# Identity copies on GpSimd, the first maxima at every fifth value step, and the SSD output steps between product and convolution, in a two-layer diffusion backbone

## The chip, the cores and the metric

The kernel runs on one core of a Trainium2 chip. A core has a matrix engine (TensorE, PE in the profile; its weight loads are PEld), a vector engine (VectorE, DVE), an engine for activations (ScalarE, ACT), a general engine (GpSimd, POOL) and one that issues most DMAs (SyncE, SP). Each works through its own queue of instructions in order and waits on semaphores for the others. The metric is the device time of one execution in microseconds.

## The reference

One batch of 512 latent tokens and 256 context tokens, width 1024, passes through two layers. Every sub-layer is preceded by an RMS norm and an adaptive shift and scale, and closed by a gate, all from a condition vector.

```python
h_l = modulate(rms_norm(x, norm_mix_w[i]), mod_l[0], mod_l[1])
...
o_l, o_c = attention_mixer(h_l, h_c, ...)     # layer 0
o_l, o_c = mamba2_mixer(h_l, h_c, ...)        # layer 1
x = x + mod_l[2] * o_l
h_l = modulate(rms_norm(x, norm_ffn_w[i]), mod_l[3], mod_l[4])
x = x + mod_l[5] * conv_ffn(h_l, ...)
```

Layer 0 mixes by attention: 16 query heads of 64 on 4 key heads, norm on queries and keys, softmax over latent and context keys. Layer 1 mixes by a Mamba-2 state-space scan (SSD) in both directions, with 8 groups of 4 heads and a state of 128:

```python
xbc = silu(dwconv_centred(xbc, conv_w, conv_b))      # 5 taps; x, B and C
states = einsum('bcsgn,bcsgrp->bcgrpn', bc, xw)      # per chunk of 128 tokens
cb = einsum('bcqgn,bcsgn->bcqsg', cc, bc)
w = cb[..., None] * decay * dtc[:, :, None]
y = einsum('...', w, xc) + einsum('bcqgn,bcgrpn->bcqgrp', cc, h_in) * exp(acs)
y = y + d_skip * xs;  out = rms_norm(y * silu(z), norm_w) @ w_out
```

Each layer ends with a gated feed-forward network with a convolution of width 3.

## The kernel before

Activations lie transposed, channels on the 128 partitions and the 768 tokens along the free axis. Every fp32 product is three matmuls on a high and a low half of each operand (`mm3`, lines 99 to 109: high by high L105, high by low L106, low by high L108). `load_w` (L90 to L96) fetches a weight tile by a DMA from SP (L95, `wst`), rounds it on ScalarE (L85, `wh`) and subtracts on VectorE or GpSimd (L87, `wl`); these tiles share a pool of ten buffers, so about three loads are under way. PSUM has two double banks (`S`) and four banks (`Bank`) that all products share: a product can start when the reader of the bank's former content is done.

Each engine's order is set by the tile framework: instructions are ranked by their place in the program and put on their engine when their operands are planned to be ready; a block at the start of attention (`manual_schedule`) keeps PE, ScalarE and VectorE in program order. DMAs are issued by SP in its own order.

**Start.** SP issues X (four DMAs, L1254), the parameters, the modulation weights (L122), the first weight slabs (L412) and the constants `cst` (L421). PE warms up (L431). ScalarE squares the eight tiles of X (L435), VectorE adds them (L437), PE sums over partitions (L236, `ssa`), an inverse root follows (L239 to L247, `rba`), PE spreads it over partitions with the identity from `cst` (L253, `rsTa`), the tokens are modulated (L281, `ht`; L290 and L291, `hha` and `hla`), and the first slab matmul `ps_l` starts. The modulation comes from `ps_ada` (L128). Slabs are split into `wsh` (ScalarE) and `wsl` (GpSimd).

**Attention, first maxima.** Softmax subtracts a bound: the maxima of the scores per query. `maxima` (L586 to L621) computes them for a pair of heads in seven steps: matmuls `ps_m` (L596), a reduction on VectorE (L598), and at the end minima `mz` (L614) and a diagonal matrix `diag` (L619), made with the two copies `id2` of the identity (L576). The scores `ps_s` (L668) then get the bound by one more matmul, `diag` by ones (L670), and go to ScalarE's exponential (L671). For the first pair, the steps of `maxima` are interleaved with the matmuls of the values (`ps_v`, L515; three per step `i` of the loop at L727). For the later pairs they are interleaved with the scores of the pair before.

**SSD.** For each of eight groups, `inproj` (L959 to L978) makes, one after the other, two tiles of x, then B, C and two of z: a product over 8 blocks (`gemm`, `ps_in`), and for x, B and C `conv`: ScalarE copies the product to `raw` (L947, L949) and makes the middle tap with bias (L950), VectorE adds four taps (L952), ScalarE applies SiLU (L953). `core` (L984 to L1105) does the group's scan as a generator: transposes of x (`ps_xt`, L992) and of B (L999), weighting (`xw`, L1006), `ps_cb` (L1037) and first state (`ps_st`, L1018), DMAs of decay rows (`E`, L1050) with exponentials on ScalarE (L1055, L1057) and products on GpSimd and VectorE (L1059, L1061, L1067), the other states, and then for each of two halves `pr` an output step: DMAs `ec` (L1076), `ps_yo` (L1083), its product with `ec` on VectorE (L1085), an add on GpSimd (L1086), `ps_y` (L1092), its reading by VectorE (L1095, into the tile `xf`), the sum (L1096), the gate (L1097, `z`), the square (L1099) and its sum (L1103). The loop at L1108 advances the group before (`prev`) while the present one is projected: its remaining states and E products after the first x, output step 0 after the B convolution, output step 1 after the C convolution; the present group's own `core` starts behind that.

Of the kernel before, what the change touches and what calls it, by code (L numbers as in the profile page):

```python
# [11 lines left out]
ALU = mybir.AluOpType  # L12
AX = mybir.AxisListType
PSUM = bass.MemoryType.PSUM
# [4 lines left out]
C = 256  # L19
# [48 lines left out]
def t3(g, name, dt=F32, n=T):  # L68
    return g.t3p.tile([P, n], dt, tag="t3", bufs=g.n3, name=name)
# [232 lines left out]
def S(g, name):  # L302
    return g.ps.tile([P, 1024], F32, tag="S", bufs=2, name=name)


def Bank(g, name):
    return g.ps.tile([P, 512], F32, tag="B", bufs=4, name=name)
# [71 lines left out]
def attention(g, fill, X, late):  # L379


    nc, I = g.nc, g.I
    S64 = slice(0, 64), slice(64, 128)
    Bk, Sb = (lambda name: Bank(g, name)), (lambda name: S(g, name))
    t2 = lambda name, dt=F32: g.t3p.tile([P, 512], dt, tag="t2", bufs=6, name=name)
# [115 lines left out]
    raw = [t3(g, f"raw{j}") for j in range(6)]  # L501
# [71 lines left out]
    nc.scalar.copy(onesr, g.ones)  # L573
    id2 = g.const.tile([P, HD], F32, name="id2")
    for h in S64:
        nc.scalar.copy(id2[h], g.ident[h, h])  # L576
    small = lambda name, dt=F32: g.p.tile([P, 2, T // P], dt, tag="mx", bufs=4, name=name)

    class Pair:
# [109 lines left out]
    for n, j in enumerate((0, 1, 2, 4, 5, 3)):  # L689
        ps = Bk("ps_c")  # L690
# [34 lines left out]

    m = pairs[0].maxima()
    for i, _ in enumerate(vals):  # L727
        if i % 6 == 5:
            next(m, None)
            next(qgen[1], None)  # L730
    for _ in m:
        pass
# [1 line left out]
    for p in range(NH // 2):  # L734
        m = iter(())
        if p < 7:
# [3 lines left out]
            m = pairs[p + 1].maxima()  # L740
# [129 lines left out]
def ssd(g, x, norm, wf, bg, close):  # L870


    nc, I, tc = g.nc, g.I, g.tc
    par = lambda name, j, rows=P: g.par[:rows, PC[name] + j : PC[name] + j + 1]
    h = norm.h
# [11 lines left out]
    t3 = lambda g, nm, dt=F32: g.t3p.tile([P, TW], dt, tag="t3", bufs=g.n3, name=nm)  # L887
    t2 = lambda nm, dt=F32, n=512: g.t3p.tile([P, n], dt, tag="t2", bufs=39, name=nm)
    small = lambda nm, shape: g.t3p.tile(shape, F32, name=nm)
    tok = lambda t: slice(t * P + (2 if t >= 4 else 0), (t + 1) * P + (2 if t >= 4 else 0))  # L890
    def gemm(w, streams):
        ps = S(g, "ps_in")
        for _ in gemm_in(g, [(ps, w)], h, (0, L), [[(i, 0, (L, C)[i])] for i in streams]):
            pass
        return ps
# [3 lines left out]
    ps = ps_dt  # L899
# [27 lines left out]
    for i in range(0, P, H2):  # L927
        f, b = slice(i, i + 32), slice(i + 32, i + 64)
# [11 lines left out]
            nc.vector.memset(r[:, c0 : c0 + 2], 0.0)  # L940
    raw_n = [0]

    def conv(ps, j, both, cv):
        raw = raws[raw_n[0] % 2]
        raw_n[0] += 1
        n = TW if both else L
        nc.scalar.copy(raw[:, 2 : 2 + L], ps[:, :L])  # L947
        if both:
            nc.scalar.copy(raw[:, L + 4 : L + 4 + C], ps[:, L:T])  # L949
        nc.scalar.activation(cv, raw[:, 2 : 2 + n], AF.Identity, scale=par("sw2", j), bias=par("sb", j))  # L950
        for tap in (0, 1, 3, 4):
            nc.vector.scalar_tensor_tensor(cv, raw[:, tap : tap + n], par(f"sw{tap}", j), cv, ALU.mult, ALU.add)  # L952
        follow(g, nc.scalar.activation(cv, cv, AF.Silu))  # L953
        return cv

# [3 lines left out]
    def inproj(gi):  # L959

        G = Group()
        ld = lambda i: load_w(g, I["win"][6 * gi + i])
        G.x = []
        for j in range(2):
            ps = ps_x0 if gi == j == 0 else gemm(ld(j), (1, 0))
            G.x.append(conv(ps, 2 * gi + j, True, t3(g, "xf")))
            yield G
        G.B = conv(gemm(ld(2), (1, 0)), 16 + gi, True, t3(g, "Bf"))
        yield G
        G.C = conv(gemm(ld(3), (0,)), 24 + gi, False, t2("Cf"))  # L970
        yield G
        G.z = []
        for j in range(2):
            ps = gemm(ld(4 + j), (0,))
            z = t2("z")
            follow(g, nc.scalar.activation(z, ps[:, :L], AF.Silu))
            G.z.append(z)
            yield G  # L978
# [5 lines left out]
    def core(gi, G):  # L984
# [25 lines left out]
        st = []  # L1010
# [58 lines left out]
        for pr in range(2):  # L1069

            ec = []
            for d in range(2):
                e = t2("ec")
                for k in range(2):
                    row = d * 32 + 4 * gi + 2 * pr + k
                    nc.sync.dma_start(e[64 * k : 64 * k + 64], ead[row : row + 1, :].broadcast_to([64, L]))  # L1076
                ec.append(e)
            for d in range(2):
                po = Bank(g, "ps_yo")
                for c in range(4):  # L1080
                    s = st[3 - c if d else c]
                    c0 = d * 256 + pr * P
                    nc.tensor.matmul(po[:, c * P : (c + 1) * P], s[:, c0 : c0 + P], G.C[:, c * P : (c + 1) * P],  # L1083
                                     start=True, stop=True)
                nc.vector.tensor_tensor(ec[d], ec[d], po, ALU.mult)  # L1085
            nc.gpsimd.tensor_tensor(ec[0], ec[0], ec[1], ALU.add)  # L1086
            py = Bank(g, "ps_y")
            for c in range(4):
                cs = slice(c * P, (c + 1) * P)
                for e in range(2):  # L1090
                    r = 2 * pr + e
                    nc.tensor.matmul(py[64 * e : 64 * e + 64, cs], xt[:, c, r * HD : (r + 1) * HD], W[r][:, cs],  # L1092
                                     start=True, stop=True)
            y = G.x[pr][:, :L]
            nc.vector.scalar_tensor_tensor(y, y, par("sd", 2 * gi + pr), py, ALU.mult, ALU.add)  # L1095
            nc.vector.tensor_tensor(y, y, ec[0], ALU.add)  # L1096
            nc.vector.tensor_tensor(G.z[pr], G.z[pr], y, ALU.mult)  # L1097
            sq = t2("ysq")
            nc.scalar.activation(sq, G.z[pr], AF.Square)  # L1099
            if acc[0] is None:  # L1100
                acc[0] = sq
            else:
                nc.gpsimd.tensor_tensor(acc[0], acc[0], sq, ALU.add)  # L1103
            gated.append(G.z[pr])
            yield  # L1105

    prev = iter(())
    for gi in range(8):  # L1108
        for i, G in enumerate(inproj(gi)):
            if i in (0, 2, 3):  # L1110
                next(prev, None)
            if gi == 0 and i == 3:
                nt = T // P
                acsT, dtT = small("acsT", [P, nt, H2]), small("dtT", [P, nt, H2])
                for src, dst in ((acs, acsT), (dt, dtT)):
                    pt = Bank(g, "ps_dtT")[:, : nt * H2]
                    for t in range(nt // 2):
                        nc.tensor.transpose(pt[:, t * P : (t + 1) * P], src[:, t * P : (t + 1) * P], g.ident)
                    nc.vector.tensor_copy(dst.rearrange("p (a c) h -> p c a h", a=2),
                                          pt.rearrange("p (c a h) -> p c a h", c=nt // 2, a=2))  # L1120

                pe = Bank(g, "ps_end")
                for d, row in ((0, P - 1), (1, 0)):
                    nc.tensor.matmul(pe[:, d * nt * 32 : (d + 1) * nt * 32], g.ident[:, row : row + 1].broadcast_to([P, P]),
                                     acsT[:, :, d * 32 : (d + 1) * 32], start=True, stop=True)
                pev = pe[:, : nt * H2].rearrange("p (d t h) -> p d t h", d=2, t=nt)

                dec = small("dec", [P, 4, 2, 32])
                steps = [(5, 4)] + [(i, 3 - i) for i in range(3)]
                for i, (tf, tb) in enumerate(steps):  # L1130
                    follow(g, nc.scalar.activation(dec[:, i, 0], pev[:, 0, tf], AF.Exp))
                    follow(g, nc.scalar.activation(dec[:, i, 1], pev[:, 1, tb], AF.Exp))

                dw = small("dw", [P, nt, H2])
                for d in range(2):
                    hs = slice(d * 32, d * 32 + 32)
                    nc.vector.tensor_tensor(dw[:, :, hs], pev[:, d], acsT[:, :, hs], ALU.subtract)
                follow(g, nc.scalar.activation(dw, dw, AF.Exp))
                nc.vector.tensor_tensor(dw, dw, dtT, ALU.mult)

                for d, t in enumerate((4, 5)):
                    hs = slice(d * 32, d * 32 + 32)
                    nc.vector.tensor_tensor(dw[:, t, hs], dw[:, t, hs], dec[:, 0, d], ALU.mult)
                nacs = small("nacs", [P, 4, H2])
                nc.vector.tensor_scalar(nacs, acsT[:, :4], -1.0, None, ALU.mult)
            if i == 3:
                cur = core(gi, G)
            if i >= 3:
                next(cur)
        prev = cur  # L1150
# [25 lines left out]
    po = [S(g, "ps_wo") for _ in range(2)]  # L1176
# [10 lines left out]
    for kp in range(8):  # L1187
        w = load_w(g, I["wout0"][kp])
        if kp == 4:
            ws, ps = wm(4), Bank(g, "ps_wo")  # L1190
# [19 lines left out]
    for m in range(4, KT):  # L1210
# [5 lines left out]
        for seg in SEGS[0] if m == KT - 1 else [(0, 0, L)]:  # L1216
            _, a, b = seg
            if m > 4:
                ps = Bank(g, "ps_wo")[:, : b - a]
# [10 lines left out]
    first = first_tiles(g, wf, nxt, bg)  # L1230
# [195 lines left out]
```

## Time and profile before

| | us |
|---|---|
| runs | 1956.39, 1950.32, 1954.3 |
| median | 1954.3 |
| profiled execution | 1954.1 |
| its span, first to last instruction | 1952.0 |
| PE busy | 1890.7 |
| VectorE, ScalarE, GpSimd busy | 1343.8, 825.4, 295.6 |

The profiled execution's clock of TensorE was 0.987 of full speed in the mean. In the views below, a timeline row gives start, duration, engine, line, operation, the tile written and the tiles read, and in brackets how long the engine had been idle before and what ended that. A row of waits gives total, number and longest. A row of windows gives for a stretch its length, then the busy time of PE, PEld, VectorE, ScalarE and GpSimd with the number of instructions, the granted clock, the share of the DMA engines, and GB/s.

### The profile page before, as it was taken

The page shows a single profiled execution, that of the slowest core. Times are in us where ns is not written, and L with a number is a line of the kernel's source. Part 1 is how long each engine was busy: PE and PEld are TensorE (multiplying, and loading weights), DVE is VectorE, ACT ScalarE, POOL GpSimd, SP SyncE. Part 2 cuts the span into 40 slices and gives each one's busy share as a digit, 9 for nine tenths or more (in the row PEclk, how much of TensorE's full clock was granted, in tenths as well). Part 3 has the DMA queues.
Part 4 walks back from the last instruction along what each step waited for, and adds up shares of the span by engine and source line. Part 5 has one row for each costly group of instructions (what it writes and reads, how often), then busy time and mean ns, then how long its engine had stood idle before and what let it go on. Part 6 is the DMA issues. An engine that isn't in the chain of part 4 may idle for free.

```text
span 1952.0 us, 27591 instructions
## 1 busy us (share of the span) xinstructions
PE 1890.7 (97%) x10844; PEld 1555.9 (80%) x10844; DVE 1343.8 (69%) x1994; ACT 825.4 (42%) x1428; POOL 295.6 (15%) x272
## 2 busy tenths in 40 slices
PE   6999999999999999999999999999999999999999
PEld 5776554678888888888888888878888888888887
DVE  4478777767777777775588876667878465555555
ACT  3444443345222222222256776665667253333331
POOL 1332110022000000000040333332335210000000
PEclk8989999999999999999999999999999999999999
DMA  8221316103333444421123334343254322323332
GB/s 330 67 80 53 119 63 215 44 23 143 127 127 123 130 130 130 130 82 60 65 87 99 102 119 120 108 119 106 78 162 121 107 69 94 98 97 97 98 97 87
DMA packets 73425, 210.02 MB, mean 108 GB/s; under 512 B 8912, under 2 KB 14416, under 8 KB 73168
## 3 DMA queue, kind: packets, MB, share of 16 engines
q1 hardware_dynamic: 73296, 208.26, 33.4%
q8 instruction: 85, 1.39, 0.3%
q14 instruction: 44, 0.36, 0.1%
HBM read 198.79 MB, written 6.82 MB: 105 GB/s over the span
## 4 chain that ended last, share of the span: by engine, by line
PE 66%; DVE 15%; issue 6%; POOL 3%; DMA 3%; ACT 2%; SPq 1%; POOLq 0%; DVEq 0%; ACTq 0%
PE ps_up L105 10%; PE ps_up L106 10%; PE ps_up L108 10%; PE ps_d L105 6%; PE ps_d L108 6%; PE ps_d L106 6%; DVE xf L952 2%; PE ps_s L668 2%; PE ps_o L632 2%; DVE E L1061 1%; DVE Bf L952 1%; DMA E<-ad 1%; DVE wl L87 1%; DVE ht L281 1%; PE ps_wo L105 1%
## 5 line engine op out<-in xcount | busy, mean ns | idle before, releaser
L87 DVE TENSOR_TENSOR wl<-wst,wh 128x1024 fp32r<-128x1024 f32 x205 | 254.0, 1239 | 276.2 <-PE ps_up L106 119.7
L85 ACT CAST wh<-wst 128x1024 fp32r<-128x1024 f32 x211 | 221.0, 1048 | 434.8 <-DMA wst<-in_wup 327.7
L106 PE MATMUL ps_up<-hlf,wh 128*128 128x512 f32 x1008 | 357.0, 354 | 0.0
L105 PE MATMUL ps_up<-hhf,wh 128*128 128x512 f32 x1008 | 357.0, 354 | 0.0
L108 PE MATMUL ps_up<-hhf,wl 128*128 128x512 f32 x1008 | 356.8, 354 | 0.0
L105 PEld LDWEIGHTS ps_up<-hhf,wh 128*128 128x128 f32 x1008 | 190.5, 189 | 26.2
L106 PEld LDWEIGHTS ps_up<-hlf,wh 128*128 128x128 f32 x1008 | 190.6, 189 | 26.1
L108 PEld LDWEIGHTS ps_up<-hhf,wl 128*128 128x128 f32 x1008 | 190.5, 189 | 26.1
L105 PE MATMUL ps_in<-hhs,wh 128*128 128x512 f32 (+1 forms) x560 | 206.0, 368 | 0.0
L108 PE MATMUL ps_in<-hhs,wl 128*128 128x512 f32 (+1 forms) x560 | 201.1, 359 | 0.0
L106 PE MATMUL ps_in<-hls,wh 128*128 128x512 f32 (+1 forms) x560 | 200.3, 358 | 0.0
L105 PE MATMUL ps_d<-hdh,wh 128*128 128x512 f32 (+1 forms) x568 | 193.9, 343 | 1.0 <-DVE X L778 0.8
L108 PE MATMUL ps_d<-hdh,wl 128*128 128x512 f32 (+1 forms) x568 | 193.5, 341 | 0.0
L106 PE MATMUL ps_d<-hdl,wh 128*128 128x512 f32 (+1 forms) x568 | 193.0, 340 | 0.3 <-DVE hdl L87 0.3
L778 DVE SCALAR_TENSOR_TENSOR X<-ps_d,mod,X 128x512 f32<-128x512 f32 (+1 forms) x240 | 132.4, 583 | 22.2 <-PE ps_d L108 21.8
L105 PEld LDWEIGHTS ps_in<-hhs,wh 128*128 128x128 f32 x560 | 107.1, 191 | 15.3 <-issue 1.2
L106 PEld LDWEIGHTS ps_d<-hdl,wh 128*128 128x128 f32 x568 | 106.7, 188 | 15.4 <-DVE hdl L87 0.7
L108 PEld LDWEIGHTS ps_in<-hhs,wl 128*128 128x128 f32 x560 | 106.8, 191 | 15.2
L105 PEld LDWEIGHTS ps_d<-hdh,wh 128*128 128x128 f32 x568 | 106.3, 188 | 15.1 <-DVE X L778 1.3
L106 PEld LDWEIGHTS ps_in<-hls,wh 128*128 128x128 f32 x560 | 107.0, 191 | 13.9
L167 DVE SCALAR_TENSOR_TENSOR junk<-wada,cb 128x1024 f32<-128x1024 f32 x96 | 116.6, 1215 | 1.1 <-ACT cb L159 0.9
L108 PEld LDWEIGHTS ps_d<-hdh,wl 128*128 128x128 f32 x568 | 106.7, 188 | 13.3
(340 smaller groups left out, 3523.7 us busy)
## 6 DMA issues: line engine op xcount, KB each, us to landing
wst<-in_wup SPq DMA_DIRECT2D x88, 512.0 KB, 3.6
wada<-in_adaT SPq DMA_DIRECT2D x48, 512.0 KB, 3.5
wst<-in_win SPq DMA_DIRECT2D x48, 512.0 KB, 3.7
wst<-in_wdown SPq DMA_DIRECT2D x44, 512.0 KB, 4.2
wada<-in_adaB SPq DMA_DIRECT2D x32, 512.0 KB, 5.0
E<-ad SPq DMA_DIRECT2D x64, 256.0 KB, 6.9
ec<-ead SPq DMA_DIRECT2D x64, 128.0 KB, 4.4
wst<-in_wout SPq DMA_DIRECT2D x16, 512.0 KB, 3.6
```

Source lines behind the costliest of these rows:

```text
L85: keep(nc.scalar.copy(hi, src))
L87: keep(eng.tensor_tensor(lo, src, _r(hi), ALU.subtract))
L105: mm(out, wh, ah, start=first, stop=False)
L106: mm(out, wh, al, start=False, stop=False)
L108: mm(out, wl, ah, start=False, stop=last)
L167: g.tc.keep_in_program_order(nc.vector.scalar_tensor_tensor(junk, w, 1.0, cb[:, v * D : (v + 1) * D], ALU.mult, ALU.mult, accum_out=md[:, ...
L281: nc.vector.scalar_tensor_tensor(t[:, c0:c1], ap, g.moda[layer][ca][:, m, v : v + 1], rs[:, c0:c1], ALU.mult, ALU.mult)
L632: nc.tensor.matmul(po[S64[e], :n], v, pr[:, 512 * e + off : 512 * e + off + n], start=first, stop=last)
L668: nc.tensor.matmul(outs[e], a[S64[e], k], b[S64[e], q], start=i == 0, stop=False)
L778: nc.vector.scalar_tensor_tensor(ap, o[:, c0:c1], gate[:, m, v : v + 1], ap, ALU.mult, ALU.add)
L952: nc.vector.scalar_tensor_tensor(cv, raw[:, tap : tap + n], par(f"sw{tap}", j), cv, ALU.mult, ALU.add)
L1061: nc.vector.tensor_tensor(E[0], E[0], E[1], ALU.add)
```

## The change

Three edits. First, the two copies of the identity (L576) go from ScalarE to GpSimd. Second, the steps of the first pair's maxima are taken at every fifth step of the values, from the first on, and no longer at every sixth; the steps of the query preparation stay at every sixth. Third, in the SSD `inproj` stops between product and convolution of B and of C as well, and the output steps of the group before are taken there. The VectorE instructions of these steps that read PSUM are collected in `late`, and the next tap of a convolution that is written gets them as predecessors in VectorE's order (no semaphore).

```diff
     for h in S64:
-        nc.scalar.copy(id2[h], g.ident[h, h])
+        nc.gpsimd.tensor_copy(id2[h], g.ident[h, h])
...
     for i, _ in enumerate(vals):
+        if i % 5 == 0:
+            next(m, None)
         if i % 6 == 5:
-            next(m, None)
             next(qgen[1], None)
...
         for tap in (0, 1, 3, 4):
-            nc.vector.scalar_tensor_tensor(cv, raw[:, tap : tap + n], par(f"sw{tap}", j), cv, ALU.mult, ALU.add)
+            i = nc.vector.scalar_tensor_tensor(cv, raw[:, tap : tap + n], par(f"sw{tap}", j), cv, ALU.mult, ALU.add)
+            while late:
+                g.tc.add_manual_dep(i.ins, late.pop().ins.name, mybir.DependencyInfo(
+                    mybir.DependencyClass.NoSync, mybir.DependencyReason.DATA), reason="PSUM first")
...
-        G.B = conv(gemm(ld(2), (1, 0)), 16 + gi, True, t3(g, "Bf"))
-        yield G
-        G.C = conv(gemm(ld(3), (0,)), 24 + gi, False, t2("Cf"))
-        yield G
+        for name, i, st in (("B", 2, (1, 0)), ("C", 3, (0,))):
+            ps = gemm(ld(i), st)
+            yield None
+            setattr(G, name, conv(ps, 8 * i + gi, i == 2, t3(g, "Bf") if i == 2 else t2("Cf")))
+            yield G
...
-                nc.vector.tensor_tensor(ec[d], ec[d], po, ALU.mult)
+                late.append(nc.vector.tensor_tensor(ec[d], ec[d], po, ALU.mult))
...
-            nc.vector.scalar_tensor_tensor(y, y, par("sd", 2 * gi + pr), py, ALU.mult, ALU.add)
+            late.append(nc.vector.scalar_tensor_tensor(y, y, par("sd", 2 * gi + pr), py, ALU.mult, ALU.add))
...
-        for i, G in enumerate(inproj(gi)):
-            if i in (0, 2, 3):
+        i = -1
+        for G in inproj(gi):
+            if G is None:
+                next(prev, None)
+                continue
+            i += 1
+            if i == 0:
                 next(prev, None)
```

On ScalarE, at the start of the program; `id` are the two copies, `acc` and `sql` the squares of X:

```order
 L573 CAST onesr<-ones 128x128
-L576 COPY id_731<-cst 64x64 x2
 L435 ACTIVATE acc<-X 128x512
 L435 ACTIVATE sql<-X 128x512 x7
```

On GpSimd, at the start of the program after the change; the second `ISA` is the library instruction, `wsl` the low half of a slab:

```order
L1428 MEMSET const-uint8-127 128x1
L1434 UNCONDITIONAL_BRANCH
L576 COPY id_731<-cst 64x64 x2
L87 ISA
L87 TENSOR_TENSOR wsl<-wst,wsh 128x768 x6
```

The copies left the place ahead of the squares and stand ahead of GpSimd's library instruction and its first `wsl`.

On PE in attention, before: the last maxima matmuls of the first pair, with value matmuls around them (18 of them between `ps_m` and `ps_s`):

```order
L515 MATMUL ps_v<-wh,hla_1_121 128x256
L596 MATMUL ps_m<-kh_948,qh 128x256 x4
L515 MATMUL ps_v<-wh,hha_2_122 128x256
...
L515 MATMUL ps_v<-wh,hla_7_133 128x256
L668 MATMUL ps_s<-qh,kh_948 128x512 x2
L668 MATMUL ps_s<-qh,kl_949 128x512 x2
L668 MATMUL ps_s<-ql,kh_948 128x512 x2
L670 MATMUL ps_s<-diag_1221,onesr 128x512 x2
```

The same place after (51 value matmuls between `ps_m` and `ps_s`):

```order
L515 MATMUL ps_v<-wh,hla_6_115 128x256
L596 MATMUL ps_m<-kh_948,qh 128x256 x4
L515 MATMUL ps_v<-wh,hha_7_116 128x256
...
L515 MATMUL ps_v<-wh,hla_7_133 128x256
L668 MATMUL ps_s<-qh,kh_948 128x512 x2
L668 MATMUL ps_s<-qh,kl_949 128x512 x2
L668 MATMUL ps_s<-ql,kh_948 128x512 x2
L670 MATMUL ps_s<-diag_1184,onesr 128x512 x2
```

The maxima stand 33 value matmuls earlier; from `ps_s` on the order is the same.

On VectorE in a steady SSD group, before, from the second half of B's taps to the weighting; the `xf` row with `ps_y` is output step 1 reading its PSUM bank:

```order
L952 SCALAR_TENSOR_TENSOR Bf<-raw_9472,par,Bf 128x770
L87 TENSOR_TENSOR wl<-wst,wh 128x1024
L952 SCALAR_TENSOR_TENSOR Bf<-raw_9472,par,Bf 128x770
L952 SCALAR_TENSOR_TENSOR Cf<-raw_9473,par,Cf 128x512 x2
L1095 SCALAR_TENSOR_TENSOR xf<-xf,par,ps_y 128x512
L952 SCALAR_TENSOR_TENSOR Cf<-raw_9473,par,Cf 128x512
L87 TENSOR_TENSOR wl<-wst,wh 128x1024
L952 SCALAR_TENSOR_TENSOR Cf<-raw_9473,par,Cf 128x512
L1085 TENSOR_TENSOR ec<-ec,ps_yo 128x512 x2
L1096 TENSOR_TENSOR xf<-xf,ec 128x512
L1097 TENSOR_TENSOR z<-z,xf 128x512
```

The same place after (one more `wl` stands some rows above it):

```order
L87 TENSOR_TENSOR wl<-wst,wh 128x1024
L955 SCALAR_TENSOR_TENSOR Bf<-raw_9472,par,Bf 128x770
L1102 SCALAR_TENSOR_TENSOR xf<-xf,par,ps_y 128x512
L1092 TENSOR_TENSOR ec<-ec,ps_yo 128x512 x2
L1103 TENSOR_TENSOR xf<-xf,ec 128x512
L1104 TENSOR_TENSOR z<-z,xf 128x512
L87 TENSOR_TENSOR wl<-wst,wh 128x1024
L955 SCALAR_TENSOR_TENSOR Cf<-raw_9473,par,Cf 128x512 x2
L1013 TENSOR_TENSOR xw<-xt,dw 128x512
L955 SCALAR_TENSOR_TENSOR Cf<-raw_9473,par,Cf 128x512
```

Output step 1 stands ahead of all taps of C instead of between them, and the taps of C are mixed with the weighting `xw`. On SP one weight load moves from ahead of the second group's E rows to behind them, and so for all later groups. PE's order in the SSD is the same but for the place of the x transposes, which stand one matmul earlier.

More of the change, by code (lines that the diff above doesn't have):

```diff
@@ L941, in ssd @@
     raw_n = [0]
+    late = []
     def conv(ps, j, both, cv):
```

## The prediction

> **What bounds the kernel now.** I read the page first, then the waits of PE, then each place where PE stood, instruction by instruction, with the granted clock around it.
>
> ```profile
> PE 1890.7 (97%) x10844; PEld 1555.9 (80%) x10844; DVE 1343.8 (69%) x1994; ACT 825.4 (42%) x1428; POOL 295.6 (15%) x272
> PE ps_xt L992 <- DVE xf L1095: 13.8, 6, 3.8
> PE ssa L236 <- DVE qn L440: 12.3, 1, 12.3
> PE ps_s L670 <- DVE diag L619: 3.6, 3, 3.1
> PE ps_first L106 <- POOL hlf L288: 2.8, 5, 1.0
> ```
>
> PE is busy for 97% of the span, so without removing matmuls only two things can shorten this kernel: PE's waits, and the stretches at a lower clock. The last four lines are the longest waits (us in total, times, longest one). The first three are the places that the three edits touch; the fourth and all smaller ones are not touched. The profiled execution took 1954.1 us, 2.1 more than its span; the median of the runs is 1954.3, so I sum against 1954.1 and take the result for the median. About 0.3% (6 us) is what a measurement of this kernel can tell from no change.
>
> **Start: the identity copies leave ScalarE.** The timeline of the first 30 us (start, duration, engine, line, in brackets the idle time before and who ended it), and two groups of DMAs with the median from issue to landing last:
>
> ```profile
> 0.74 1.98 SPq L1254 DMA_DIRECT2D X<-in_xT  x4
> 7.45 2.40 SPq L122 DMA_DIRECT2D wada<-in_adaA  x3
> 13.90 0.50 ACT L576 COPY id<-cst 64x64 f32<-64x64 f32 x2 [11.58 <-DMA cst<-in_cst]
> 14.41 0.63 ACT L435 ACTIVATE acc<-X 128x512 f32<-128x512 f32 x1
> 14.94 3.73 ACT L435 ACTIVATE sql<-X 128x512 f32<-128x512 f32 x7
> 15.59 5.47 DVE L437 TENSOR_TENSOR acc<-acc,sql 128x512 f32<-128x512 f32 x7 [14.32 <-ACT sql L435]
> 21.12 1.87 PE L236 MATMUL ssa<-ones,acc 128*128 128x1 f32 x8 [12.26 <-DVE qn L440]
> 24.46 1.99 POOL L87 TENSOR_TENSOR wsl<-wst,wsh 128x768 fp32r<-128x768 f32 x1 [24.02 <-ACT wsh L85]
> 24.83 1.11 PE L253 MATMUL rsTa<-cst,rba 128*128 128x128 f32 x4
> 26.37 1.07 PE L128 MATMUL ps_ada<-wada,sc 128*32 128x256 f32 x16
> 28.49 0.49 PE L105 MATMUL ps_l<-hha,wsh 128*128 128x512 f32 x1 [1.05 <-ACT hha L290]
> 29.64 0.63 PE L108 MATMUL ps_l<-hha,wsl 128*128 128x512 f32 x1
> 12.00:26.00 14.00, 4.88 (x30) 3.54 (x31) 7.02 (x16) 5.99 (x14) 1.54 (x1) 0.52 1.05 389
> X<-in_xT SPq DMA_DIRECT2D x4, 512.0 KB, 5.1
> wada<-in_adaA SPq DMA_DIRECT2D x11, 384.0 KB, 8.1
> ```
>
> ScalarE stands until 13.90 for the constants. Behind its two copies stand, one after the other, the squares of X, their sum on VectorE (ends at 15.59 + 5.47 = 21.06), the row sums `ssa` on PE, the norm and the first slab matmul at 28.49. X itself came long before: four DMAs, issued from 0.74 to 2.72; with the median of 5.1 the first piece is there at about 5.8 and the last at 7.8. Without the copies the first add can start two squares later, at 5.8 + 0.63 + 0.53 (3.73 / 7) = 7.0 by that median, a little over 1 us sooner if the first piece, alone on the queues, lands faster than the median; seven adds of 0.78 (5.47 / 7) then end between 11.3 and 12.5. The last piece with its two squares and one add would allow 9.7, so the adds decide. I take 11.5: 21.06 - 11.5 = **9.6 us earlier**, bounds 8.5 and 10.5.
>
> What is late next? The constants hold the identity for the transposes `rsTa` too; they land at 13.9, and `rsTa` moves to 24.83 - 9.6 = 15.2. The second block of modulation weights, issued from 7.45 to 9.85, lands by about 9.85 + 8.1 = 18.0 at the latest; its matmuls move to 26.37 - 9.6 = 16.8, and the slab behind them to 18.9, so they may be up to 1 us late: that is in the bounds. The clock was 0.52 from 12 to 26; I assume that the moved work meets the same (a gain of up to 3 otherwise).
>
> On GpSimd the copies now wait for 13.9 instead, ahead of a library instruction that has no row, and ahead of `wsl`. That `wsl` is wanted by the third slab matmul, at 29.64 - 9.6 = 20.0; with 1.99 for itself it must start by 18.0. The copies are done at 13.9 + 1.0 (twice ScalarE's 0.50) = 14.9, so 3 us are left for the library. Its price lies between zero and a delay that eats all 9.6; I take zero, since this row of the trace shows `wsl` starting without delay behind the same instruction, though there it had long idle time. Term: **-9.6**.
>
> **The first maxima.** The chain of waits (first row), the timeline and the windows, 115 to 142 us:
>
> ```profile
> 115.68 2.35 PE ps_v L515 x18
> 124.04 1.22 DVE L598 TENSOR_REDUCE mb<-ps_m 128x4 f32<-128x1024 f32 x1 [1.55 <-PE ps_m L596]
> 129.25 1.03 DVE L619 TENSOR_TENSOR diag<-id,mz 128x384 fp32r<-128x384 f32 x2
> 130.33 0.50 PE L670 MATMUL ps_s<-diag,onesr 64*128 64x512 f32 x2 [3.11 <-DVE diag L619]
> 132.00:142.00 10.00, 10.00 (x43) 5.82 (x46) 7.57 (x12) 5.93 (x10) 3.61 (x3) 0.50 0.29 85
> ```
>
> When the last maxima matmul is done (124.04) VectorE needs until 130.3 for reduction, minima and diagonal: 6.3 us. PE has 18 value matmuls left for that time (2.35 us as in the first row) and six score matmuls, then stands 3.11. In the new order 51 value matmuls follow the last maxima; 33 more at 0.13 (2.35 / 18) are 4.3 us of cover against 3.1 of wait, which goes whole. The last row says that PE, never idle from 132 to 142, had half its clock there: up to 5 us lost. ScalarE's exponentials between the matmuls would keep some of it, so I take 4 (bounds 0 and 5). Moving the maxima forward costs PE nothing: their number is the same, and `diag` is ready early. Term: 3.1 + 4 = **-7** (bounds -3 and -8).
>
> **SSD.** One of the six places on PE, VectorE, ScalarE and SP; then windows of the clock, the first behind this wait, the others the first and the last of three groups:
>
> ```profile
> 1237.67 6.40 SPq L1050 DMA_DIRECT2D E<-ad  x8
> 1260.61 0.36 ACT L949 COPY raw<-ps_in 128x256 f32<-128x256 f32 x1
> 1263.68 2.07 DVE L952 SCALAR_TENSOR_TENSOR xf<-raw,par,xf 128x770 f32<-128x770 f32 x2
> 1282.05 1.52 DVE L952 SCALAR_TENSOR_TENSOR Cf<-raw,par,Cf 128x512 f32<-128x512 f32 x2
> 1283.50 0.74 DVE L1095 SCALAR_TENSOR_TENSOR xf<-xf,par,ps_y 128x512 f32<-128x512 f32 x1
> 1284.29 1.09 PE L992 MATMUL ps_xt<-cst,xf 128*128 128x128 f32 x8 [3.78 <-DVE xf L1095]
> 1284.82 1.22 DVE L87 TENSOR_TENSOR wl<-wst,wh 128x1024 fp32r<-128x1024 f32 x1
> 1297.28 1.05 PE L1037 MATMUL ps_cb<-Cf,Bf 128*128 128x128 f32 x8
> 1284.00:1290.00 6.00, 5.71 (x22) 4.74 (x23) 4.58 (x7) 3.07 (x5) 1.28 (x1) 0.72 0.01 3
> 1265.70:1324.10 58.40, 54.62 (x319) 47.21 (x318) 42.91 (x49) 38.33 (x82) 21.02 (x19) 0.97 0.38 109
> 1382.80:1442.00 59.20, 56.97 (x330) 49.33 (x329) 42.51 (x49) 39.66 (x83) 21.25 (x19) 0.97 0.40 114
> ```
>
> PE's order hardly changes; VectorE's does. PE stands for the PSUM bank that VectorE frees at 1283.50 + 0.74, and this reading of `ps_y` stood behind two taps of C (1.52). Now they stand behind it, but one more `wl` (1.22) ahead. The E rows, issued at 1237.67 behind weights that wait for PE, now have one weight load fewer ahead of them, so VectorE's work on E ends sooner, and the x taps (1263.68) can start when the second x is copied (1260.61 + 0.36), up to 2.7 earlier; I count 2.5. Net 1.5 - 1.2 + 2.5 = 2.8 us earlier. The waits of the first list are 13.8 / 6 = 2.3 in the mean and 3.8 at most, so 2.8 would leave about 1 us of all six. But next the taps of C are just in time (rival 1); I leave 0.6 a group, 3.6, and gain 10.2 (bounds 3 and 13.8). In three groups in a row the mean clock was 0.97: 0.03 x 58.8 = 1.7 us each, 5.1 in all, which goes with the waits (bounds 0 and 5.1). GpSimd's and ScalarE's orders shift too, at 21 and 38 us of a group's 58 off the path. Term: **-15** (bounds -3 and -19).
>
> [...]
>
> **Sum.** 9.6 + 7 + 15 = 31.6; 1954.1 - 31.6 = 1922.5, say **1922**. Nothing later takes it back: PE is the bound behind each place, and the DMA engines are busy for 0.38 and 0.40 of the quoted groups.
>
> **Rivals.**
> (1) The SSD wait moves. The taps of C now stand behind y (0.74), two `ec` products, an add of GpSimd, x + ec, z, a `wl` whose buffer PE frees, and partly `xw`; laid out by such rows they end with their silu near 1292.5, while PE, relieved of 3.8 + 1.7, wants `ps_cb` at 1297.28 - 5.5 = 1291.8. For it: no slack. Against: only tenths are missing. At 2 us a group more C gives 3: 1934. Chance 0.17.
> (2) The library instruction takes over 12 us behind the constants and the start gives nothing: 1932. For: no row prices it; against: that is six times the longest GpSimd operation quoted here. Chance 0.08.
> [...]
>
> ```profile
> 1342.76 0.44 PE L992 MATMUL ps_xt<-cst,xf 128*128 128x128 f32 x2 [2.07 <-DVE xf L1095]
> 1401.41 0.87 PE L992 MATMUL ps_xt<-cst,xf 128*128 128x128 f32 x4 [2.23 <-DVE xf L1095]
> 1220.30 2.30 DVE L87 TENSOR_TENSOR wl<-wst,wh 128x1024 fp32r<-128x1024 f32 x1
> 1220.18 1.33 POOL L1103 TENSOR_TENSOR ysq<-ysq 128x512 f32<-128x512 f32 x1 [3.69 <-ACT ysq L1099]
> ```
>
> [...] Chance 0.08.
> (4) Slower: VectorE falls behind at `ps_cb`. The last two rows show a `wl` of 2.30 instead of 1.22 beside an add of GpSimd; the new order puts GpSimd's adds beside VectorE's work from y to the taps of C, about 11 us. If half of that were slowed so, PE would wait some 3.8 us in each of seven groups with 1.7 of half clock behind it: 1922 + 7 x 5.5 = 1960. From there on it is slower. But two adds of 1.3 us a group can slow 3 us of it at most. Chance 0.05. [...]
>
> **Numbers.** The forecast 0.56, its own range 1912 to 1931; rivals (1) to (3) 0.17, 0.08 and 0.08; two of them together, near 1944, 0.04; all three, no change, 0.02; slower 0.05. So faster 0.93, same 0.02, slower 0.05. The range takes in the forecast and the first three rivals with some spread, 1911 to 1940.
>
> **What would show it.** Right: ScalarE's first square near 5, `ssa` near 11.5, the first slab matmul near 19; no wait for `diag`, and clock 1.0 in the 10 us behind it; waits of PE in the SSD under 5 us in all, a group of 55 to 56 us instead of 58.5. Wrong: `wsl` starting after 18, `ps_cb` or `ps_xt` collecting over a microsecond a group, or half clock where no wait is left.

## The result and the profile after

The changed kernel took 1919.4 us in the median (1918.2 to 1920.1) against 1952.3 for the kernel before (four runs now, one more than in the table above): ratio 0.983, interval 0.981 to 0.986, 33 us less. The forecast was 1922 in a range from 1911 to 1940. The profiled execution of the changed kernel took 1919.1 us (span 1917.3), 35.0 less than the one before.

The first reading is by stages, from the first or last matmul of a tile on PE in the two traces, by their starts (us):

| from - to | before | after | difference |
|---|---|---|---|
| start - first `ps_v` | 101.6 | 92.8 | -8.8 |
| first `ps_v` - first `ps_q` (the first maxima lie here) | 54.0 | 49.2 | -4.8 |
| first `ps_q` - last `ps_s` | 252.1 | 250.4 | -1.7 |
| last `ps_s` - first `ps_in` (end of attention, FFN 0) | 622.3 | 621.6 | -0.7 |
| first `ps_in` - last `ps_y` (SSD) | 470.8 | 452.3 | -18.5 |
| last `ps_y` - last `ps_d` (projection, FFN 1) | 447.6 | 447.4 | -0.2 |

The page and the waits of PE after the change; the three waits that headed the list before (13.8, 12.3 and 3.6) are now 1.8, 3.5 and 0.5:

```profile
PE 1879.9 (98%) x10844; PEld 1547.5 (81%) x10844; DVE 1335.1 (70%) x1994; ACT 824.2 (43%) x1426; POOL 313.0 (16%) x274
PE ssa L236 <- DVE qn L440: 3.5, 1, 3.5
PE ps_xt L999 <- DVE xf L1102: 1.8, 6, 0.5
```

PE's busy time fell by 10.8 us with the same number of matmuls. That is the other source of the gain: matmuls that used to run at half clock, above all in the SSD (5.3 us less, with three half-clock stretches of 3.4 us before and none after) and the first maxima (3.6 less, with 10.2 us of half clock before and 3.4 after).

The start after the change, from the timeline:

```profile
4.65 0.63 ACT L435 ACTIVATE acc<-X 128x512 f32<-128x512 f32 x1 [2.32 <-DMA X<-in_xT]
8.38 3.08 DVE L437 TENSOR_TENSOR acc<-acc,sql 128x512 f32<-128x512 f32 x4 [0.25 <-ACT sql L435]
11.51 1.87 PE L236 MATMUL ssa<-ones,acc 128*128 128x1 f32 x8 [3.48 <-DVE qn L440]
14.01 0.51 POOL L576 COPY id<-cst 64x64 f32<-64x64 f32 x2 [13.57 <-DMA cst<-in_cst]
14.92 2.02 POOL L87 TENSOR_TENSOR wsl<-wst,wsh 128x768 fp32r<-128x768 f32 x1 [0.40 <-POOL id L576]
19.13 0.79 PE L105 MATMUL ps_l<-hha,wsh 128*128 128x512 f32 x1 [0.19 <-ACT hha L290]
```

The first square runs when the first piece of X has landed (4.65), the sum is done at 11.46, and the first slab matmul comes at 19.13 instead of 28.49. The library instruction between the copies and `wsl` took no more than the 0.40 us of the idle time in the fifth row.

The first maxima, VectorE and PE, and the clock behind them:

```profile
112.54 0.70 DVE L614 TENSOR_TENSOR mz<-ma,mb 64x6 f32<-64x6 f32 x4
113.27 1.03 DVE L619 TENSOR_TENSOR diag<-id,mz 128x384 fp32r<-128x384 f32 x2
117.94 0.39 PE L670 MATMUL ps_s<-diag,onesr 64*128 64x512 f32 x2
122.30 1.75 PE L236 MATMUL ssq<-cst,qsq 128*128 128x2 f32 x12 [0.95 <-ACT qsq L523]
124.00:127.00 3.00, 3.00 (x13) 0.64 (x16) 3.00 (x4) 0.86 (x3) 0.00 (x0) 0.53 0.68 206
```

`diag` is ready 3.6 us before PE wants it. The four minima `mz` took 0.70 us; in the kernel before they took 3.92. And there is still a stretch of half clock, some 3.4 us long instead of ten, behind a wait of 0.95.

One SSD group after the change: SP, VectorE, PE, and the windows of that group:

```profile
1211.00 5.63 SPq L1057 DMA_DIRECT2D E<-ad  x8
1217.47 1.89 PE L1025 MATMUL ps_st<-xw,Bt 128*128 128x256 f32 x8
1240.76 1.02 DVE L955 SCALAR_TENSOR_TENSOR xf<-raw,par,xf 128x770 f32<-128x770 f32 x1
1259.66 0.74 DVE L1102 SCALAR_TENSOR_TENSOR xf<-xf,par,ps_y 128x512 f32<-128x512 f32 x1
1260.45 0.66 PE L999 MATMUL ps_xt<-cst,xf 128*128 128x128 f32 x4 [0.24 <-DVE xf L1102]
1269.82 0.74 DVE L955 SCALAR_TENSOR_TENSOR Cf<-raw,par,Cf 128x512 f32<-128x512 f32 x1
1271.65 1.05 PE L1044 MATMUL ps_cb<-Cf,Bf 128*128 128x128 f32 x8
1217.20:1272.50 55.30, 55.06 (x330) 47.78 (x330) 41.53 (x49) 38.29 (x83) 23.24 (x20) 1.00 0.40 116
```

Counted from the first state matmul (1217.47), the E rows go out 6.5 us ahead of it, the first x tap comes at 23.3, VectorE reads `ps_y` at 42.2, and PE waits 0.24 for it. The last tap of C ends 1.1 us ahead of `ps_cb` (SiLU comes between and ends 0.4 ahead of it), which doesn't wait. PE is busy for 55.06 of 55.30 us, at full clock.

### The profile page after: what moved, and what is told of

The parts are those of the page before. It is cut to its first block, busy times and chain, and to the rows that moved or that the text cites. A ratio compares the mean times of both kernels' runs of the same rounds, so it can differ in the third digit from the quotient of the medians.

```text
span 1917.3 us, 27562 instructions
## 1 busy us (share of the span) xinstructions
PE 1879.9 (98%) x10844; PEld 1547.5 (81%) x10844; DVE 1335.1 (70%) x1994; ACT 824.2 (43%) x1426; POOL 313.0 (16%) x274
## 4 chain that ended last, share of the span: by engine, by line
PE 79%; DVE 8%; issue 4%; ACT 2%; POOL 2%; DMA 1%; SPq 0%; DVEq 0%; POOLq 0%; ACTq 0%
PE ps_up L106 10%; PE ps_up L108 10%; PE ps_up L105 10%; PE ps_d L105 6%; PE ps_d L108 6%; PE ps_d L106 6%; PE ps_in L108 4%; PE ps_in L106 4%; PE ps_in L105 4%; PE ps_o L632 2%; PE ps_s L668 2%; PE ps_st L1025 2%; DVE ht L281 1%; PE ps_wo L108 1%; PE ps_wo L105 1%
```

## The experiments

Twelve kernels, each timed beside the kernel before on its own chip, in three batches on three chips. Their stages, as in the table above:

```
            first ps_l  first ps_v  maxima  attention  FFN 0   SSD   end
before         28.5       101.6      54.0     252.1    622.3  470.8  447.6
after          19.1        92.8      49.2     250.4    621.6  452.3  447.4
only_a         18.0        92.0      55.1     252.1    628.6  468.5  446.5
only_b         28.6       102.0      49.4     252.9    627.7  469.5  446.2
only_c         28.6       100.4      54.4     253.8    626.5  452.1  447.1
c_lean         18.6        92.5      50.6     250.1    624.9  452.3  447.3
c_half         18.2        92.2      48.3     253.7    621.8  468.7  446.5
pad2           18.5        92.2      50.5     254.9    621.9  465.5  446.1
pad4           18.2        88.8      53.1     252.0    621.5  481.2  447.0
max6           18.9        92.8      48.6     253.8    622.2  452.4  447.4
warm36         18.2        90.7      53.3     251.5    621.9  452.1  447.5
wq_dve         28.6       100.3      57.0     251.6    621.9  468.0  446.7
cst_first      19.9        92.4      56.4     251.8    622.1  470.2  446.7
best1          18.2        91.3      54.1     253.8    621.8  452.2  447.3
```

The SSD column shows how well a stage can be read: every kernel with the old order has 468.0 to 470.8, every one with the new order 452.1 to 452.4. The column of the maxima is wider by half-clock windows: six kernels with the same attention code (after, c_lean, c_half, pad2, pad4, warm36) have 48.3 to 53.3, and four with the old one (before, only_a, only_c, cst_first) 54.0 to 56.4.

**only_a**, the first edit alone.

> The kernel before with the first edit alone: the identity copies on GpSimd. Theory (each edit's gain is local, waits and the clock behind them): the first slab matmul near 19.1 instead of 28.5, 9 us less than the kernel before (0.4 to 0.5%), and the six SSD waits (13.8 us) with their three half-clock windows stay as they were. Rival (what the clock does behind a wait depends on where the wait falls in time): the same waits, but shifted by 9.4 us another number of them is followed by half clock, none to six instead of three, so the gain lies anywhere between 4 and 14 us.

Measured: 1945.7 us, ratio 0.996 (0.994 to 0.997), 9 us less. The start gave 9.6, the SSD kept its waits and three half-clock windows. The theory holds. Its FFN 0 is 6 us longer than before, which the edit doesn't aim at: PE is idle there for 2 us more, above all waiting for slow GpSimd instructions (last section), and busy for 4 us more (614.1 against 610.0), with 13.7 us of half clock where the kernel before has none.

**only_b**, the second edit alone.

> The kernel before with the second edit alone: the first maxima at every fifth step. Theory: the wait of 3.1 us for diag is gone, two of three half-clock windows behind it too, the matmuls from the third score tile on 5.5 us earlier: 5 to 7 us less than before. Rival (the wait is hidden by the fill work of the later pairs, which is then late): 0 to 2 us.

Measured: 1950.9 us, ratio 0.997 (0.995 to 0.999). The wait for `diag` is gone and the stage of the maxima went from 54.0 to 49.4, 4.6 less. That is a little under the 5 to 7 expected, and the whole is 3.9 faster; FFN 0 was long here too.

**only_c**, the third edit alone.

> The kernel before with the third edit alone: the SSD output steps between product and convolution. Theory: PE's waits for ps_xt under 3 us in all, no half clock from 1040 to 1500, the last ps_y some 17 us earlier: 16 to 19 us less than before. Rival (part of the SSD gain came from the shifted start, not from the order): 10 to 13 us.

Measured: 1940.7 us, ratio 0.993 (0.991 to 0.995). The SSD takes 452.1, 18.7 less than before, without the shifted start, and PE's waits for `ps_xt` are 1.8: the theory holds in the trace of that stage. The whole is only 14 us faster, between the 16 to 19 of the theory and the 10 to 13 of the rival, again with a longer FFN 0 and attention. Stage by stage, against the trace of the kernel before, the three edits alone give 9.6 + 4.6 + 18.7 = 32.9, the 33 us of the change. By the medians on this batch's chip they give 9.1 + 3.9 + 14.1 = 27, where c_lean (next) gained 31; the 4 us between stay open, since the kernel before was not traced on that chip.

**c_lean**: how much of the third edit is needed?

```diff
         for name, i, st in (("B", 2, (1, 0)), ("C", 3, (0,))):
             ps = gemm(ld(i), st)
-            yield None
+            if i == 3:
+                yield None
...
-            while late:
-                g.tc.add_manual_dep(...)
...
-            if i == 0:
+            if i in (0, 2):
                 next(prev, None)
```

> The changed kernel with a smaller third edit: only the output step of C lies between product and convolution, that of B stands behind B's convolution as before, and no tap is held back by the list of PSUM readers. Theory (VectorE's read of ps_y in output step 1 is the whole matter): same time as the changed kernel, within 2 us, waits for ps_xt 1 to 3 us in all. Rival (the held-back taps do the work): the read of ps_y slides behind two taps again and 10 to 17 us come back.

Measured: 1923.6 us, ratio 0.984 (0.982 to 0.987), the same as the whole change within the intervals; SSD 452.3. PE's waits there:

```profile
PE ps_xt L997 <- DVE xf L1100: 1.8, 6, 0.5
```

Only the step between C's product and convolution is needed. The step at B and the taps held back are not.

**c_half**: the output step of C after two of its four taps.

```diff
-        for tap in (0, 1, 3, 4):
+        for n_, tap in enumerate((0, 1, 3, 4)):
+            if mid and n_ == 2:
+                mid()                      # next(prev, None), for C alone
...
-            yield None
+            if i == 2:
+                yield None
```

> The changed kernel, but the output step of C is taken after two of C's four taps instead of ahead of all of them; all else as changed. Theory (PE's wait for ps_xt is VectorE's read of ps_y, and it is as late as the taps of C ahead of it): the read stands behind two taps again, waits for ps_xt of 10 us or more, and the time from the first product of the SSD to the last ps_y, 452.3 us in the changed kernel and 470.8 before, is 465 or more. Rival (it is enough that the step is written ahead of the end of the convolution): under 457.

Measured: 1936.9 us, ratio 0.991 (0.989 to 0.993); SSD 468.7, and the old wait:

```profile
PE ps_xt L1003 <- DVE xf L1106: 12.1, 6, 3.1
```

In this kernel the E rows go out behind as many weight loads as before, too. So it matters whether the step stands ahead of two taps or behind them. The order of the taps and the earlier E rows come and go together in this scheduler, and were not told apart by a run.

**pad2** and **pad4**: more work on VectorE ahead of the read of `ps_y`.

```diff
             y = G.x[pr][:, :L]
+            for _ in range(2 * pr):        # pad4: 4 * pr
+                late.append(nc.vector.tensor_copy(scr, py))
```

> The changed kernel with two added copies on VectorE that read the PSUM bank ps_y of output step 1 ahead of the real read (they compute nothing that is used). Theory (PE waits one for one for the release of that bank, and part of such waits is followed by half clock): the release is 1.3 us later, PE waits 1.6 instead of 0.3 us a group, 9 us more in all, and one to six half-clock windows of 1.7 us appear between 1010 and 1470; 10 to 19 us slower than the changed kernel, of which the copies' 0.7 each explain 9. [...] Rival (VectorE has slack there): under 4 us.

> The changed kernel with four instead of two added copies on VectorE that read ps_y ahead of the real read. Two copies made waits of up to 1.1 and 1.4 us in each group and no half clock in the SSD. Theory (waits of 2 to 3 us do bring half clock now and then): waits of 2 to 2.8 us at ps_xt and ps_cb, 25 to 28 us of wait in all, and two or more half-clock windows of 1.7 us between 1010 and 1490. [...]

Measured: pad2 1936.0 us, ratio 0.991 (0.989 to 0.993), SSD 465.5; pad4 1950.0 us, 0.999 (0.997 to 1.000), SSD 481.2. PE's waits in the SSD, first pad2, then pad4:

```profile
PE ps_cb L1045 <- ACT Cf L960: 9.1, 7, 1.4
PE ps_xt L1000 <- ACT xt L1001: 5.4, 6, 1.1
```

```profile
PE ps_cb L1045 <- ACT Cf L960: 19.0, 7, 4.3
PE ps_xt L1000 <- DVE ec L1093: 5.1, 6, 2.4
```

The added work costs time at once, and twice: PE waits for the transposes and, the taps of C being late as well, again at `ps_cb`. There is hardly any slack in VectorE's chain; that was rival 1 of the prediction, not reached but near. My expectation of pad2 was wrong on the place (one wait instead of two) and on the clock: with waits of up to 1.4 there is no half clock in the SSD. With four copies it is there, in three windows, as the theory of pad4 has it, each behind one of these waits on PE (24 us of them in all, the longest 4.31, where 25 to 28 and 2.8 were expected):

```profile
1111.10 1.58 PE L1045 MATMUL ps_cb<-Cf,Bf 128*128 128x128 f32 x8 [2.83 <-ACT Cf L960]
1448.09 0.66 PE L1000 MATMUL ps_xt<-cst,xf 128*128 128x128 f32 x4 [2.40 <-DVE ec L1093]
1466.31 1.78 PE L1045 MATMUL ps_cb<-Cf,Bf 128*128 128x128 f32 x8 [4.31 <-ACT Cf L960]
1450.00:1454.00 4.00, 4.00 (x13) 3.18 (x12) 3.69 (x6) 1.06 (x2) 1.28 (x1) 0.62 0.00 0
1112.00:1118.00 6.00, 6.00 (x33) 5.41 (x32) 1.22 (x1) 3.73 (x6) 3.95 (x5) 0.74 0.85 288
```

The first row of windows lies behind the wait of 2.40, the second behind the wait of 2.83. The other waits at these two places, five of them of 2.38 to 2.39, brought no half clock; what sets them apart is under "The clock" below.

**max6**: maxima at every sixth step, but from the first step on (`i % 6 == 0`).

> The changed kernel with the first maxima at every sixth step from the first on, so that 33 value matmuls instead of 51 (and 18 before) stand behind the last maxima. Theory (cover of 0.12 us per value matmul against VectorE's 6.3 us): 15 matmuls more than before take 1.8 off the wait of 3.1, PE waits 1.0 to 1.5 us for diag; the time from the first ps_v to the first ps_q, 49.2 in the changed kernel and 54.0 before, is 50.5 and 1.7 more for each half-clock window that follows. Rival (one step more of lead is enough): no wait, 49 to 50.

Measured: 1921.5 us, ratio 0.983 (0.981 to 0.985), maxima stage 48.6. No wait for `diag` at all; the rival holds. My cover was right, but VectorE's 6.3 us weren't: the minima took 0.70 (from 114.74) here too, with no GpSimd instruction beside them.

**wq_dve**: is it GpSimd that makes the minima slow in the kernel before?

```diff
-            w = load_w(g, I["wq"][p - 4], lo_engine="pool")
+            w = load_w(g, I["wq"][p - 4])
```

> The kernel before, with the low halves of the later query weights made on VectorE instead of GpSimd; nothing else. Theory (the four tiny minima mz took 3.9 us instead of 0.7 because VectorE was shut out while GpSimd ran a two-operand instruction beside them): that wl (1.2) now runs on VectorE ahead of the minima, they take 0.7 to 2.0, diag is ready 1.5 to 2.5 us earlier and PE's wait for it is 0.6 to 1.6 us instead of 3.1; first ps_v to first ps_q 50 to 52.5 instead of 54.0, half clock behind it included. Rival (the minima are slow by themselves): they take 3.9 again and the wait is 4.3.

Measured: 1954.8 us, ratio 1.001 (0.9995 to 1.003): no gain. VectorE and GpSimd at the place, and PE's wait:

```profile
123.18 1.30 POOL L529 TENSOR_TENSOR qsw<-qsw,cs 128x512 f32<-128x512 f32 x1
123.73 1.83 DVE L87 TENSOR_TENSOR wl<-wst,wh 128x1024 fp32r<-128x1024 f32 x1
125.48 1.77 DVE L614 TENSOR_TENSOR mz<-ma,mb 64x6 f32<-64x6 f32 x4
124.55 2.13 POOL L530 TENSOR_TENSOR raw<-raw,qsw 128x512 f32<-128x512 f32 x1
PE ps_s L670 <- DVE diag L619: 2.4, 1, 2.4
```

With one GpSimd instruction fewer beside them the minima fell from 3.92 to 1.77, as the theory has it, but `wl` now stands ahead of them and itself took 1.83 instead of 1.22 beside the GpSimd instruction of the first row, which ended at 124.48. The wait fell only to 2.4, not to the 0.6 to 1.6 expected, and the stage didn't gain. It doesn't speak against the theory on the minima, but it isn't a repair.

**cst_first**: the kernel before, copies on ScalarE, the constants loaded first of all.

```diff
+    nc.sync.dma_start(g.cst, I["cst"][:, :CST_COS])
     for m in range(0, KT, 2):
         nc.sync.dma_start(X[:, m : m + 2, :L], ...)
...
-    nc.sync.dma_start(g.cst, I["cst"][:, :CST_COS])     # behind the first slab
```

> The kernel before, with the identity copies still on ScalarE, but the load of the constants issued first of all instead of behind X and the first weights. Theory (ScalarE's queue stood for the constants' arrival and nothing else): the copies run at 4 to 6 us, the squares behind them, ssa at 11 to 13, the first slab matmul at 18 to 20.5 instead of 28.5; 8 to 10 us faster than the kernel before. Rival (the copies on ScalarE, or the later X, cost the start): ssa later than 14, under 6 us faster.

Measured: 1942.6 us, ratio 0.994 (0.992 to 0.996), 10.7 us less. From the timeline:

```profile
2.65 0.50 ACT L575 COPY id<-cst 64x64 f32<-64x64 f32 x2 [0.33 <-DMA cst<-in_cst]
12.37 1.83 PE L236 MATMUL ssa<-ones,acc 128*128 128x1 f32 x8 [3.53 <-DVE qn L439]
```

The copies run even earlier than the 4 to 6 us expected. The gain is the same as from moving the copies (first `ps_v` 92.4 and 92.0). So the engine of the copies is not the point; that they waited at the head of a queue is.

**warm36**: 36 warm-up matmuls instead of 24.

> The changed kernel with 36 instead of 24 warm-up matmuls, so that PE is busy up to about 11.5 us, when ssa starts, instead of 8.0. Theory (the half clock from 11 to 25 us comes from PE's idle 3.5 us ahead of ssa): full clock at ssa and on; the slab matmuls from 19 us on run at 0.23 instead of 0.43 us, and the first ps_v comes 2 to 4 us earlier; 2 to 4 us faster than the changed kernel. Rival (the sparse small matmuls from 11.5 to 19 let the clock fall all the same, or the loads, at 400 GB/s until 40 us, bind next): no more than 1 us.

Measured: 1922.8 us, ratio 0.984 (0.982 to 0.986): no gain over the change, as the rival has it. PE was busy up to `ssa`, but among the small matmuls behind it it was busy for only 2.05 of 3.41 us, and the clock fell:

```profile
10.88:14.29 3.41, 2.05 (x24) 1.39 (x24) 2.26 (x10) 1.13 (x3) 0.53 (x1) 1.00 1.04 405
14.29:17.70 3.41, 3.33 (x24) 2.27 (x24) 1.50 (x6) 0.39 (x2) 2.17 (x3) 0.50 1.04 401
```

The first `ps_v` came about 2 us earlier (90.7), which two more half-clock windows in the maxima (53.3) took back. Here, what the start gave was lost in such windows.

**best1**: the change with the maxima one value step later and `wl` of the later queries on VectorE.

> The changed kernel with the first maxima one value step later (first step at the second of the values, so that it doesn't wait for the query) and the later query weights' low halves on VectorE. Theory (1.0 us of wait for qh goes, and VectorE is not shut out beside GpSimd): 1 to 4 us faster than the changed kernel, the upper end if the half-clock window near 125 goes too. Rival (those loads on VectorE delay its other work): 0 to 3 us slower.

Measured: 1925.5 us, ratio 0.985 (0.983 to 0.988): not faster than the change. The wait for `qh` is still 1.0, so the later step doesn't remove it, and the stage took 54.1, with three half-clock windows where the change has one.

No run was faster than the change by more than its interval.

## Why the prediction was right, and where it was off

**Start, forecast 9.6, measured 9.4 to the first slab matmul and 8.8 to the first `ps_v`.** Each step is as written: squares at 4.65, `ssa` at 11.51, slab at 19.13. The adds decided, as said. cst_first shows that it was the constants' arrival, and the library of rival 2 cost 0.40 at most.

**Maxima, forecast 7, measured 4.8.** The wait of 3.1 went, as forecast. PE's idle time in the stage fell by only 1.2, since waits that come next took back 1.9: 0.9 for `qsq` and 0.7 for a reduction are new, and the wait for `qh`, which the kernel before has too, grew from 0.8 to 1.0. Their rows, the first of the kernel before, the others of the changed one:

```profile
PE ps_m L596 <- ACT qh L85: 0.8, 1, 0.8
PE ps_m L596 <- ACT qh L85: 1.0, 1, 1.0
PE ssq L236 <- ACT qsq L523: 0.9, 1, 0.9
PE ps_m L596 <- DVE ma L598: 0.7, 1, 0.7
```

The sentence "moving the maxima forward costs PE nothing" put these at nothing and was the wrong one. Of the clock 3.6 came back, near the 4 forecast: one half-clock window (1.7) is left of three (5.1), so the clock of 1.0 in the 10 us behind the scores, named as a sign, did not come. That only one is left is in part luck: with the same attention code, c_lean and pad2 show two and pad4 and warm36 three. And the cover was counted against 6.3 us of VectorE work that was only 3.0 without GpSimd beside it; the result did not hang on that, since 51 value matmuls cover either.

**SSD, forecast 15, measured 18.5.** The step held: VectorE reads `ps_y` 3.3 us earlier in the group (42.2 against 1283.50 - 1237.99 = 45.5), where 2.8 was forecast. The x taps come 2.4 earlier (23.3 against 1263.68 - 1237.99 = 25.7), and from there to the read it is 0.9 less. The forecast was 3.5 short for two reasons. It left 0.6 a group, 3.6, for the taps of C at `ps_cb`; they are in time, and the waits for `ps_xt` fell by 12.0 instead of 10.2. The other 1.4 are three waits of PE that I had not counted, in the kernel before between 1040 and 1500: `ps_xt` for `xt` (0.7), `ps_yo` for `hs` (0.5) and `ps_y` for `E` (0.2), all gone after; the last tenths are rounding. The clock gave the 5.1 forecast. Rival 1 stayed a rival, but pad2 shows how near it was.

**The sum, forecast 31.6, measured 33 to 35.** Errors of -0.8, -2.2 and +3.5 in the three terms nearly cancelled, so that the total is so close is luck. Most of the rest between the two traces is 1.7 us of attention, from a half-clock window between 193 and 197 us that the changed kernel's trace doesn't have. No edit aimed at it, and pad2 and pad4, with the attention code of the change, have one at that place (181 and 180 us).

**The clock.** The prediction gives a chance of 0.08 to its rival 3, that half clock does not follow waits as short as those here (2.07 to 3.78 us in the rows of the SSD). No run shows that. In pad4 waits of 2.40 and 2.83 are followed by 0.62 and 0.74, and in the SSD of the kernel before half clock follows waits of 2.07, 2.23 and 3.78; where the longest wait is 0.9 (after) or 1.4 (pad2) there is none. On the other side, half clock does not follow each wait over 2 us: it follows one of 2.07 in the kernel before and not one of 3.06 in wq_dve. What the traces do show is a grid in time: in each of the fourteen, the stretches of half clock last 3.41 us or a whole multiple of it (3.41, 6.83, 10.24 and 13.65 in the kernel before; those cut off by the end of the program are shorter), and begin a whole multiple apart. Here are PE's busy time and the clock in such windows, first around the wait of 2.07, then around that of 3.06:

```profile
1340.27:1343.68 3.41, 1.34 (x11) 0.92 (x9) 3.38 (x6) 2.49 (x4) 0.00 (x0) 1.00 0.47 154
1343.68:1347.10 3.42, 3.42 (x10) 2.67 (x9) 2.69 (x4) 2.41 (x4) 0.60 (x1) 0.50 0.00 0
1397.20:1400.61 3.41, 1.91 (x13) 1.25 (x9) 3.41 (x3) 1.34 (x2) 1.99 (x1) 1.00 0.46 127
1400.61:1404.02 3.41, 1.85 (x12) 1.69 (x13) 3.38 (x6) 2.77 (x5) 0.00 (x0) 1.00 0.08 31
1404.02:1407.43 3.41, 3.41 (x16) 2.77 (x15) 1.95 (x4) 1.57 (x2) 1.29 (x1) 1.00 0.00 0
```

The shorter wait lies whole in one window, the longer one is split over two. In the SSD of the fourteen traces 18 windows have PE idle for 1.90 us or more, and half clock follows each; of those with 1.88 or less it follows one, which was at half clock itself (in the kernel before it follows 2.05, 2.07 and 2.23, and not 1.83). So in the SSD of these runs half clock went with the idle time within one window, from 1.90 of 3.41 us on, and not with the length of the wait.

## What to carry to other kernels

Look first at what heads an engine's queue: here two copies (0.50 us together) that waited 11.58 us for a late load held up everything behind them, and either another queue (only_a, 9 us) or an earlier load (cst_first, 10.7 us) cured that. When a consumer must free a PSUM bank, put its read ahead of work of the same engine that nobody waits for yet (PE's waits for `ps_xt` fell from 13.8 to 1.8 us), and then look for the next wait: here the work put behind it was in time by 0.4 us. In the SSD here, half clock for 3.41 us followed 1.90 us or more of PE's idle time in one window of the clock, so by my estimate waits of that kind cost about 1.7 us (half of 3.41) more than their length. Read gains by stage, since one of these traces differs from the next by such windows.

## What the runs showed of the hardware

**VectorE beside GpSimd.** In the kernel before, the four minima of 64x6 elements took 3.92 us, in the changed one 0.70. GpSimd's rows at that place, before the change:

```profile
125.41 2.38 POOL L87 TENSOR_TENSOR wl<-wst,wh 128x1024 fp32r<-128x1024 f32 x1
127.75 1.26 POOL L530 TENSOR_TENSOR raw<-raw,qsw 128x512 f32<-128x512 f32 x1
132.91 2.37 POOL L87 TENSOR_TENSOR wl<-wst,wh 128x1024 fp32r<-128x1024 f32 x1 [3.90 <-PE ssq L236]
133.00 2.30 DVE L602 COPY mb<-ma 128x4 f32<-128x4 f32 x1
```

In the chain of waits the minima appear as 0.17 (125.30), 2.32 (125.48), 1.21 (127.82) and 0.17: the second ends at 127.80 and the third at 129.03, when the GpSimd instructions beside them end (127.79 and 129.01). So does the tiny copy in the last two rows (135.30 and 135.28). So three VectorE instructions of 64x6 and 128x4 elements, begun beside a GpSimd one, lasted until that one ended. Not each did: L239 (128x12), begun at 132.92 beside the `wl` of the third row, took 0.17. The other way round, in wq_dve GpSimd's L530, begun at 124.55 beside VectorE's `wl`, took 2.13 instead of 1.26. The 3.2 us of the minima are as long as the whole wait of 3.1 for `diag`. At their new place they have no GpSimd instruction beside them, so the wait had two reasons to go, this and the cover; max6, with less cover, has no wait either, and no run tells the two apart.

**A chip with slower GpSimd instructions.** In all four traces from the chip of the first batch single subtractions on GpSimd at the joins of the layers took up to 3.7 us, against 1.6 in the ten others (duration in ns, least, median and longest), here after the change and in only_a:

```profile
L288 POOL TENSOR_TENSOR hls<-ht,hhs x12: 729/928/1602, 979.9 to 1010.2; 128x256 fp32r<-128x256 f32 x12
L288 POOL TENSOR_TENSOR hls<-ht,hhs x12: 732/870/3682, 990.7 to 1022.3; 128x256 fp32r<-128x256 f32 x12
```

PE waited for them, up to 2.8 us at once instead of 0.8, which is part of why FFN 0 took 625 to 629 us in that batch instead of 622; half-clock windows are another. Why they were slow there stays open.

**Half clock without idle time.** Outside the SSD half clock also came with less idle time. In max6 half clock followed a window in which PE was never idle, but spent more than half of it on matmuls of two columns:

```profile
295.80 1.95 PE L134 MATMUL ps_adt<-cst,ada_sb 128*128 128x2 f32 x16
294.39:297.80 3.41, 3.41 (x29) 2.42 (x28) 2.89 (x4) 1.33 (x3) 3.33 (x3) 1.00 1.02 403
297.80:301.21 3.41, 3.41 (x14) 1.59 (x14) 3.06 (x5) 1.02 (x1) 0.88 (x1) 0.50 0.94 363
```

In warm36 the clock fell behind 1.36 us of idle time among small matmuls, and stayed at half for two windows more although PE was busy for 3.33 and 3.23 of 3.41 us. So windows in which the profile has PE busy for 3.23 to 3.41 us were followed by half clock here; why is not shown.
